# Hybrid decoder layer on one core: opening groups with sums on VectorE, one pool of slots for raw weights, h requested through ScalarE's queue, constants made later

## The chip, the core and the metric

The kernel runs on one core of a Trainium2 chip. Its matrix engine is TensorE (PE in the profile; PEld is its weight load). VectorE (DVE), ScalarE (ACT) and GpSimd (POOL) do the elementwise work, and SyncE (SP) only issues transfers. Each engine takes its instructions in the order of its own queue, and transfers that an engine issues stand in that same queue until their own waits are over. The metric is the time of one execution in microseconds, lower is better.

## The reference

One layer over 256 tokens of width 2048, all in float32: a half-step SwiGLU FFN of inner width 5632 with post-LayerNorm, a mixer (multi-head latent attention and differential attention side by side, merged by sigmoid gates), and a second FFN.

```python
h = _layer_norm(ALPHA * h + 0.5 * _swiglu(h, ffn1_w_gate, ffn1_w_up, ffn1_w_down), ln1_g, ln1_b)
mix = _mixer(h, positions, w_in, ...)
h = _layer_norm(ALPHA * h + mix, ln2_g, ln2_b)
h = _layer_norm(ALPHA * h + 0.5 * _swiglu(h, ffn2_w_gate, ffn2_w_up, ffn2_w_down), ln3_g, ln3_b)

def _swiglu(x, w_gate, w_up, w_down):
    return (jax.nn.silu(x @ w_gate) * (x @ w_up)) @ w_down
```

The mixer needs a few constants: rotary sines and cosines of the positions, a causal mask, distance biases, the scalar lambda and a scaled gain row.

## The kernel before

**Numbers.** Every float32 operand is split in two (`split`, lines 188 to 190): ACT casts it to a high part in float32r, VectorE subtracts that from the source for the low part. A product is three matmuls (`triple`, lines 245 to 248): high by high, high by low, low by high. The stationary operand is a 128x128 tile of x, the moving one 512 columns of weights.

**Units.** Weights come in units of 128x1024 floats (two k tiles of 512 columns, 512 KB). A plain unit is loaded by SP into a raw tile, split into a pair of ring tiles (`wring`), and multiplied with both blocks of 128 tokens: 12 matmuls. Up to 3 units are loaded and 4 split ahead of the one that is multiplied (`look(3, 4)`).

**Groups.** In the FFNs two column chunks, the two token blocks and, for part of the k range, two halves of k are worked by a scheme of seven block products instead of eight (`Pair.seven`). A formed unit multiplies one sum or difference of weight blocks with one sum or difference of x blocks: 6 matmuls. The weight blocks are called A and E (first chunk), B and D (second chunk); each is two units. In the kernel before A, E and D are loaded as `sraw` tiles by SP; where B has to be added, POOL issues an accumulating load of it into the tile in place (line 328), after the tile's split. Other sums are made by VectorE (line 323). The formed x blocks (`Acts.sevens`) are `minus`, a pair from the raw tile, four differences (line 168) and two more pairs.

A gate-and-up group (`group`) is 14 formed units (products 1 to 7, two units each) and 8 plain ones ((chunk, unit) with units 4 to 7). Its products meet in PSUM banks; ACT copies a bank after products 1, 6 and 5 (line 387) and after product 7 (line 392, in `third`), and the copies are combined with the plain units' banks (line 576). In an ordinary group the second half of the units (1, 4) to (1, 7) adds into bank X, which the copy in line 392 reads. Eleven groups make one FFN's gate and up. The first one, `opening=True`, has an order of its own, since x or h is only then arriving; its plain units are multiplied with block 0 at once and with block 1 up to `lag` units later.

**h.** The SwiGLU result is transposed in blocks and written to DRAM (`hT`, line 557). The down stage reads it back in quads of 512 rows (`get`, line 598, `hraw`) by POOL's queue. `seven` in the down stage asks for the quads of a formed block 16 and 14 units ahead and for the quad of its plain units 2 units ahead; `take` asks 11 units ahead.

**Order.** Functions attached by `at(i, ...)` run when unit i is multiplied, or when it is loaded if inline; `later(n, ...)` runs a function n units on. This sets the program's order; a planner then lays out each engine's queue from it by priority, so that work without open inputs can stand earlier. Tiles of 4 KB per partition come from one pool of 40 slots (`act`): ring pairs, x and h quads, sums, snapshots, z, gain rows. Raw weight tiles have a pool of their own with 4 buffers (`wpool`). Six small `tmp` slots serve the rest.

**Constants.** `setup` runs 24 units into the first FFN: it loads positions, frequencies, lambda's vectors and the gain row by POOL's queue and makes the mixer's constants from them on VectorE and ACT.

**LayerNorm.** Its constructor, at the start of a down stage, loads the residual into four z tiles and has ACT scale them 4 units later (line 488); `take_rows` loads gain and bias rows and has ACT halve the gain 4 units later (line 496).

## Time and profile before

| | us |
|---|---|
| median of 3 runs (2122.46 to 2128.14) | 2124.46 |
| profiled execution, whole | 2124.58 |
| its span, first to last instruction | 2122.7 |
| TensorE busy in the span | 2032.3 |
| VectorE busy | 1611.9 |
| ACT busy | 1231.5 |
| first FFN's gate and up | from 0 to about 512 |
| its down stage | about 512 to 754 |
| mixer and output projection | about 754 to 1377 |
| second FFN | about 1377 to 2123 |

A view's row for a group of instructions has line, engine, operation, tiles (out<-in), shape and count, then busy us, mean ns, and the idle time before with what ended it. A timeline row has start and length in us, and in brackets the idle time before and its releaser. A row of stretches has for each engine its busy time and count, then the granted TensorE clock (1.00 is full), the DMA share and GB/s. Where all four token and weight operands pass through one helper, line 189 is ACT's cast and line 190 VectorE's subtraction; tiles tell them apart (raw: plain unit, sraw: formed unit, xs: formed x, hraw: h read back).

### The profile page before, as it was taken

Reading aid. Unit: us, or ns where it says so; the run is one execution under the profiler, and the core shown is the slowest. Engines: PE = TensorE matmul, PEld = TensorE weight load, DVE = VectorE, ACT = ScalarE, POOL = GpSimd, SP = SyncE. Lnnn points to the kernel's source line nnn. Section 1 sums busy time; section 2 is a strip of 40 time slices with the busy share of each in tenths; the row PEclk is TensorE's granted clock in tenths of the full one; section 3 lists DMA queues with packets and bytes.
Section 4 is the critical chain, followed back from the end, with each engine's and each line's share of the span. In section 5 each row is a group of like instructions: output and inputs, shape, how many; then the busy total and the mean of one; then the engine's idle time right before and its main releaser. Section 6 shows DMA issues by size and latency. Waiting matters only on the chain.

```text
span 2122.7 us, 25232 instructions
## 1 busy us (share of the span) xinstructions
PE 2032.3 (96%) x8968; PEld 1659.4 (78%) x8968; DVE 1611.9 (76%) x1905; ACT 1231.5 (58%) x1569; POOL 262.2 (12%) x399
## 2 busy tenths in 40 slices
PE   7789999999999999999999999988999999999997
PEld 5678888887887788888888887866888888787875
DVE  4788888888898885455665555678888888888887
ACT  4566656666665575554674444456656566666563
POOL 1211121122101000000000000011211121221110
PEclk8899999999999999999999999999999999999999
DMA  8767888878878756544455575666888888887983
GB/s 266 188 197 235 228 255 240 236 228 307 273 263 257 243 170 215 175 159 150 168 169 189 189 269 179 215 210 185 228 255 246 233 246 251 249 286 230 290 256 126
DMA packets 135134, 475.16 MB, mean 224 GB/s; under 512 B 17424, under 2 KB 17504, under 8 KB 135008
## 3 DMA queue, kind: packets, MB, share of 16 engines
q1 hardware_dynamic: 100512, 358.13, 48.5%
q0 software_dynamic: 34496, 115.42, 23.8%
q8 instruction: 70, 1.15, 0.2%
q14 instruction: 56, 0.46, 0.1%
HBM read 455.66 MB, written 17.83 MB: 223 GB/s over the span
## 4 chain that ended last, share of the span: by engine, by line
PE 57%; DMA 13%; DVE 11%; issue 9%; ACT 4%; POOL 1%; ACTq 0%; DVEq 0%; SPq 0%; POOLq 0%
PE mm L246 18%; PE mm L248 18%; PE mm L247 18%; DVE wring L190 6%; DMA sraw<-in_gu_dram 5%; DMA hraw<-hT 3%; ACT wring L189 2%; DMA raw<-in_dn_dram 2%; DMA sraw<-in_dn_dram 1%; DVE sraw L323 1%; DMA z<-res 1%; DMA lv<-in_lam_dram 1%; POOL sraw L328 1%; DVE h L190 1%; DMA z<-in_x_dram 0%
## 5 line engine op out<-in xcount | busy, mean ns | idle before, releaser
L190 DVE TENSOR_TENSOR wring<-raw,wring 128x1024 fp32r<-128x1024 f32 (+2 forms) x502 | 601.1, 1205 | 283.3 <-ACT wring L189 282.6
L189 ACT CAST wring<-raw 128x1024 fp32r<-128x1024 f32 (+2 forms) x502 | 515.7, 1038 | 360.0 <-PE mm L248 287.4
L189 ACT CAST wring<-sraw 128x1024 fp32r<-128x1024 f32 x420 | 436.0, 1050 | 295.4 <-DVE sraw L323 101.7
L190 DVE TENSOR_TENSOR wring<-sraw,wring 128x1024 fp32r<-128x1024 f32 x420 | 504.3, 1218 | 102.2 <-ACT wring L189 100.4
L246 PE MATMUL mm<-wring,h 128*128 128x512 f32 (+2 forms) x1344 | 528.1, 393 | 13.3 <-ACT snap L392 5.5
L247 PE MATMUL mm<-wring,h 128*128 128x512 f32 (+2 forms) x1344 | 522.4, 389 | 3.6 <-DVE wring L190 3.5
L248 PE MATMUL mm<-wring,h 128*128 128x512 f32 (+2 forms) x1344 | 521.6, 388 | 0.7 <-DVE h L190 0.4
L246 PE MATMUL mm<-wring,xs 128*128 128x512 f32 x840 | 333.9, 398 | 25.9 <-ACT wring L189 13.8
L247 PE MATMUL mm<-wring,xs 128*128 128x512 f32 x840 | 335.1, 399 | 17.4 <-DVE wring L190 17.3
L248 PE MATMUL mm<-wring,xs 128*128 128x512 f32 x840 | 331.4, 395 | 1.6 <-DVE xs L190 1.5
L246 PEld LDWEIGHTS mm<-wring,h 128*128 128x128 f32 x1344 | 254.6, 189 | 68.1 <-ACT snap L392 7.9
L247 PEld LDWEIGHTS mm<-wring,h 128*128 128x128 f32 x1344 | 254.9, 190 | 56.3 <-DVE wring L190 7.1
L248 PEld LDWEIGHTS mm<-wring,h 128*128 128x128 f32 x1344 | 254.6, 189 | 53.7 <-DVE h L190 2.6
L246 PEld LDWEIGHTS mm<-wring,xs 128*128 128x128 f32 x840 | 160.3, 191 | 66.9 <-ACT wring L189 19.2
L247 PEld LDWEIGHTS mm<-wring,xs 128*128 128x128 f32 x840 | 160.8, 191 | 60.5 <-DVE wring L190 27.1
L248 PEld LDWEIGHTS mm<-wring,xs 128*128 128x128 f32 x840 | 160.6, 191 | 35.0 <-DVE xs L190 2.3
L246 PE MATMUL mm<-wring,x 128*128 128x512 f32 x352 | 139.5, 399 | 10.9 <-ACT snap L392 5.7
L323 DVE TENSOR_TENSOR sraw<-sraw,sraw 128x1024 f32<-128x1024 f32 x120 | 144.0, 1220 | 1.3 <-DMA sraw<-in_gu_dram 0.3
L328 POOL DMA_DIRECT2D sraw<-in_gu_dram x88 | 75.9, 863 | 536.0 <-DMA raw<-in_gu_dram 237.2
L247 PE MATMUL mm<-wring,x 128*128 128x512 f32 x352 | 139.2, 396 | 2.0 <-DVE wring L190 2.0
L248 PE MATMUL mm<-wring,x 128*128 128x512 f32 x352 | 138.9, 395 | 0.0
L557 POOL DMA_DIRECT2D hT<-blocks x176 | 96.9, 559 | 264.9 <-DVE blocks L555 262.1
(250 smaller groups left out, 1775.5 us busy)
## 6 DMA issues: line engine op xcount, KB each, us to landing
raw<-in_gu_dram SPq DMA_DIRECT2D x176, 512.0 KB, 4.6
sraw<-in_gu_dram SPq DMA_DIRECT2D x132, 512.0 KB, 7.0
raw<-in_dn_dram SPq DMA_DIRECT2D x112, 512.0 KB, 4.4
sraw<-in_gu_dram POOLq DMA_DIRECT2D x88, 512.0 KB, 8.0
sraw<-in_dn_dram SPq DMA_DIRECT2D x48, 512.0 KB, 6.2
hraw<-hT POOLq DMA_DIRECT2D x44, 512.0 KB, 10.1
sraw<-in_dn_dram POOLq DMA_DIRECT2D x32, 512.0 KB, 7.2
raw<-in_wgm_dram SPq DMA_DIRECT2D x32, 512.0 KB, 3.3
```

What stands on the lines that cost most here:

```text
L189: S.copy(hi, src)
L190: V.tensor_tensor(out=lo, in0=src, in1=hi.bitcast(F32), op=ALU.subtract)
L246: PE.matmul(o, xh, wh, start=first, stop=False, skip_group_check=again)
L247: PE.matmul(o, xh, wl, start=False, stop=False, skip_group_check=again)
L248: PE.matmul(o, xl, wh, start=False, stop=last, skip_group_check=again)
L323: V.tensor_tensor(out=t, in0=t, in1=self.blocks[joins[p], s], op=ALU.add)
L328: nc.gpsimd.dma_start(self.blocks[adds[p], s], self.w[1][4 * d + s], accum_op=ALU.add)
L557: nc.gpsimd.dma_start(hT[q, b].rearrange("(g r) (i f) -> i r g f", g=4, i=4)[i], t[32 * i:32 * (i + 1), :].rearrange("r (g f) -> r g f", g=4))
```

## The change

- Opening groups (both FFNs): B is loaded by SP into two tiles of its own, and VectorE adds it into A before product 5 and into D before product 7; no accumulating loads there. Six plain units come first, then products mixed with the two others. Just before product 1 all delayed block-1 products are made (`together`, `lag` 0), and x's formed blocks and the later x loads move by one to four units.
- Ordinary groups: product 7 and the unit (0, 7) change places, and the second of the four outputs is finished by that unit and no longer by `third`.
- Raw tiles come from the common pool, now 44 slots; `wpool` and its 4 buffers are gone.
- `get` is issued by ACT instead of POOL, 18, 16 and 8 units ahead for formed blocks and their plain units, 16 for `take`.
- z is scaled 16 units after its load in the FFNs and 5 in the mixer's end, the gain rows 10 units after.
- `setup` runs at the start of the first FFN's second half of down; it keeps the mask and issues all loads, and `constants` makes the rest 16 units later.

```diff
@@ -29,7 +29,7 @@
 G = 2
-SLOTS = 40
+SLOTS = 44
 LAG = 5
@@ -62,7 +62,6 @@
     const = ctx.enter_context(tc.tile_pool(name="const", bufs=1))
-    wpool = ctx.enter_context(tc.tile_pool(name="wpool", bufs=1))
     apool = ctx.enter_context(tc.tile_pool(name="apool", bufs=1))
@@ -267,7 +266,7 @@
             def load():
-                st["raw"] = wpool.tile([P, G * width], F32, tag="raw", name=nm("raw"), bufs=4)
+                st["raw"] = act_tile([P, G * width], F32, "raw")
                 nc.sync.dma_start(st["raw"], w[j])
@@ -303,11 +302,14 @@
 
-        def seven(self, d, p, then=None):
+        def seven(self, d, p, then=None, by_dma=True):
             fresh = {1: ("A", 0, 0), 2: ("E", 0, 2), 3: ("D", 1, 2)}
...
             joins = {6: "D", 4: "E"}
-            adds = {1: "A", 6: "D"}
+            adds = {1: "A", 6: "D"} if by_dma else {}
+            if not by_dma:
+                fresh[5] = ("B", 1, 0)
+                joins.update({5: "B", 7: "B"})
 
@@ -347,7 +349,7 @@
             def load():
-                st["raw"] = wpool.tile([P, 1024], F32, tag="raw", name=nm("raw"), bufs=4)
+                st["raw"] = act_tile([P, 1024], F32, "raw")
                 nc.sync.dma_start(st["raw"], self.w[n][j])
@@ -394,16 +396,14 @@
                 done(0, 0, bk["Y"], n1, ALU.subtract)
-            done(0, 1, bk["W"], n3, ALU.subtract)
-            if opening:
+                done(0, 1, bk["W"], n3, ALU.subtract)
                 done(1, 0, bk["Z"], n2, ALU.add)
...
         def last0(b):
-            if b == 0:
-                done(0, 0, bk["Y"], st["t"][0], ALU.subtract)
+            done(0, b, bk["YW"[b]], st["t"][2 * b], ALU.subtract)
 
@@ -412,13 +412,13 @@
         if opening:
-            seq = [(0, 4), (0, 5), (1, 4), (1, 5), (0, 6), 1, (1, 6), 2, (0, 7), 5, (1, 7), 3, 6, 4, 7]
+            seq = [(0, 4), (0, 5), (1, 4), (1, 5), (0, 6), (1, 6), 1, (0, 7), 2, (1, 7), 5, 3, 6, 4, 7]
         else:
-            seq = [1, 2, (0, 4), 5, (0, 5), 3, 6, (0, 6), 4, (0, 7), 7, (1, 4), (1, 5), (1, 6), (1, 7)]
+            seq = [1, 2, (0, 4), 5, (0, 5), 3, 6, (0, 6), 4, 7, (0, 7), (1, 4), (1, 5), (1, 6), (1, 7)]
         items = []
...
             if isinstance(i, int):
-                items += pr.seven(0, i, thens.get(i))
+                items += pr.seven(0, i, thens.get(i), not opening)
             else:
@@ -485,7 +485,7 @@
                     nc.gpsimd.dma_start(t, residual[b, :, h * 1024:(h + 1) * 1024])
-                    later(4, lambda t=t: S.mul(t, t, ALPHA))
+                    later(16 if scale < 1.0 else 5, lambda t=t: S.mul(t, t, ALPHA))
             self.rows = (g, bt)
@@ -493,7 +493,7 @@
             for t in self.gb[0]:
-                later(4, lambda t=t: S.mul(t, t, 0.5))
+                later(10, lambda t=t: S.mul(t, t, 0.5))
 
@@ -585,7 +585,12 @@
                            lambda n_, b, bank, snap, op, p=p: sum_done(2 * p + n_, b, bank, snap, op), p == 0)
-        for i, f in zip((5, 7, 10, 11, 13), x.sevens(0)):
+        def together():
+            lag[0] = 0
+            catch_up(0)
+
+        at(6, together)
+        for i, f in zip((6, 8, 11, 12, 13), x.sevens(0)):
             at(i, f)
@@ -595,13 +600,13 @@
         def get(i, q):
-            nc.gpsimd.dma_start(hx[i].raw(q), hT[q].rearrange("b p f -> p b f"))
+            nc.scalar.dma_start(hx[i].raw(q), hT[q].rearrange("b p f -> p b f"))
 
...
         def take(i, q):
-            at(len(items) - 11, lambda: get(i, q))
+            at(len(items) - 16, lambda: get(i, q))
             for b in range(2):
@@ -649,11 +654,11 @@
                 t = len(items)
-                at(t - 16, lambda: get(i, 2 * d))
-                at(t - 14, lambda: get(i, 2 * d + 1))
+                at(t - 18, lambda: get(i, 2 * d))
+                at(t - 16, lambda: get(i, 2 * d + 1))
                 for k, f in enumerate(hx_forms(i, d)):
                     at(t - 7 + k, f)
-                at(t - 2, lambda: get(i, q))
+                at(t - 8, lambda: get(i, q))
                 for b in range(2):
@@ -679,6 +684,8 @@
             else:
+                if n == 1:
+                    at(len(items), setup)
                 items += lone(4)
@@ -728,12 +735,20 @@
         nc.gpsimd.dma_start(pos_i, a["pos_col"])
+        row_i = tmp_tile([P, T], "row_i", I32)
+        nc.gpsimd.dma_start(row_i, a["pos_row"].partition_broadcast(P))
+        invf = tmp_tile([P, HALF], "invf")
+        nc.gpsimd.dma_start(invf, a["inv_freq"].partition_broadcast(P))
+        lv = tmp_tile([P, 4, P], "lv")
+        nc.gpsimd.dma_start(lv.rearrange("p a n -> p (a n)"), a["lam"].partition_broadcast(P))
+        nc.gpsimd.dma_start(subg, a["subln_g"].partition_broadcast(P))
+        later(16, lambda: constants(pos_i, row_i, invf, lv))
+
+    def constants(pos_i, row_i, invf, lv):
         pos = sm(2, "pos")
...
         V.tensor_scalar(out=npos, in0=pos, scalar1=-1.0, scalar2=None, op0=ALU.mult)
-        row_i = tmp_tile([P, T], "row_i", I32)
-        nc.gpsimd.dma_start(row_i, a["pos_row"].partition_broadcast(P))
         row = tmp_tile([P, T], "posrow")
@@ -743,8 +758,6 @@
 
-        invf = tmp_tile([P, HALF], "invf")
-        nc.gpsimd.dma_start(invf, a["inv_freq"].partition_broadcast(P))
         ang = tmp_tile([P, 2, 2, HALF], "ang")
@@ -763,8 +776,6 @@
 
-        lv = tmp_tile([P, 4, P], "lv")
-        nc.gpsimd.dma_start(lv.rearrange("p a n -> p (a n)"), a["lam"].partition_broadcast(P))
         lp = tmp_tile([P, 2, P], "lp")
@@ -774,7 +785,6 @@
         V.tensor_scalar(out=lam, in0=ld, scalar1=LAMBDA_INIT, scalar2=None, op0=ALU.add)
-        nc.gpsimd.dma_start(subg, a["subln_g"].partition_broadcast(P))
         V.tensor_scalar(out=subg, in0=subg, scalar1=0.5 * (1.0 - LAMBDA_INIT), scalar2=None, op0=ALU.mult)
@@ -1044,10 +1054,9 @@
     def first(at):
-        for i, q, b in ((0, 2, 0), (1, 2, 1), (4, 3, 0), (4, 3, 1), (5, 0, 0), (5, 0, 1), (5, 1, 0), (5, 1, 1)):
+        for i, q, b in ((0, 2, 0), (1, 2, 1), (4, 3, 0), (4, 3, 1), (6, 0, 0), (8, 1, 0), (8, 1, 1), (9, 0, 1)):
             at(i, lambda q=q, b=b: load_x(q, b), True)
 
-    later(24, setup)
     set_ring(LAG + 5)
...
```

## Prediction

> **What bounds the kernel now.** I read the page's engine shares first, then the stretches, then the waits of TensorE, then the timelines of the holes.
>
> ```profile
> span 2122.7 us, 25232 instructions
> PE 2032.3 (96%) x8968; PEld 1659.4 (78%) x8968; DVE 1611.9 (76%) x1905; ACT 1231.5 (58%) x1569; POOL 262.2 (12%) x399
> 300.00:350.00 50.00, 50.00 (x222) 41.42 (x221) 43.80 (x48) 31.79 (x38) 11.84 (x20) 1.00 0.80 230
> 25.00:50.00 25.00, 17.56 (x51) 11.43 (x52) 13.64 (x14) 10.19 (x12) 1.74 (x2) 0.73 0.70 202
> 50.00:75.00 25.00, 20.08 (x78) 15.04 (x78) 21.95 (x21) 16.46 (x20) 3.36 (x4) 0.93 0.63 175
> 75.00:100.00 25.00, 17.43 (x65) 13.16 (x64) 19.12 (x31) 11.55 (x16) 7.83 (x13) 0.85 0.79 215
> 100.00:125.00 25.00, 20.48 (x73) 15.97 (x72) 18.49 (x35) 15.81 (x18) 0.00 (x0) 0.81 0.53 149
> 1400.00:1425.00 25.00, 21.93 (x92) 17.18 (x91) 20.31 (x21) 15.47 (x17) 1.68 (x2) 0.98 0.84 272
> 1425.00:1450.00 25.00, 22.56 (x86) 17.56 (x85) 19.49 (x22) 16.50 (x20) 1.69 (x2) 0.89 0.59 133
> 1450.00:1475.00 25.00, 20.27 (x77) 15.39 (x78) 21.04 (x22) 11.93 (x13) 6.17 (x10) 0.93 0.71 212
> ```
>
> The columns after the stretch are its length, then busy time and count on PE, PEld, DVE, ACT and POOL, then the granted clock, the DMA share and GB/s. A steady stretch holds 222 matmuls in 50 us, one per 0.225 us: there TensorE is the bound and nothing but fewer matmuls would help, and the change keeps their number. So the time that can move is in stretches with fewer matmuls. Against 111 per 25 us, the stretches from 25 to 125 us lack 60, 33, 46 and 38, which at 0.225 us is 13.5, 7.4, 10.4 and 8.6 us; those from 1400 lack 19, 25 and 34 (4.3, 5.6, 7.7 us). A hole costs more than its width: the granted clock falls to 0.73 to 0.93 with it.
>
> **The change, part by part.** The sum is made against the profiled execution, 2124.58 us, which is the span and 1.9 us around it; the median of the runs shown, 2124.46, is the same.
>
> *a. The third snapshot no longer stands before a matmul.* In an ordinary group the copy of bank X (line 392) is followed at once by the unit (1,4), whose second half adds into X. The new order puts the 12 matmuls of (0,7) between.
>
> ```profile
>   PE mm L246: 11.2, 6
> 497.26 0.39 PE L248 MATMUL mm<-wring,x 128*128 128x512 f32 x1
> 501.59 0.50 PE L246 MATMUL mm<-wring,x 128*128 128x512 f32 x1 [3.94 <-ACT snap L392]
> 502.56 0.63 PE L246 MATMUL mm<-wring,x 128*128 128x512 f32 x1
> 505.11 0.63 PE L246 MATMUL mm<-wring,x 128*128 128x512 f32 x1
> 490.81 1.06 ACT L488 ACTIVATE z<-z 128x1024 f32<-128x1024 f32 x1 [3.25 <-DMA z<-in_x_dram]
> 498.77 1.05 ACT L488 ACTIVATE z<-z 128x1024 f32<-128x1024 f32 x1
> 500.96 0.58 ACT L392 COPY snap<-mm 128x512 f32<-128x512 f32 x1
> ```
>
> The first row is from the view of line 392: TensorE lost 11.2 us to it in 6 waits. In the longest one shown, six matmuls from 502.56 to 505.11 then took 2.55 us, 1.2 us over pace; two such long waits (the second FFN repeats the first's code) make at most 11.2 + 3 = 14. The copy came late because ACT stood 3.25 us for the residual tile z and then scaled four of them at about 1.06 us each. These scalings move from 4 units to 16 units behind the load, out of the last group, so 7 us of what kept ACT late goes too. What is late next is the cast of the following unit, right behind the copy on ACT. Gain 3 (that cast takes the place) to 14; I take 11, since both causes go.
>
> *b. Constants leave the first FFN's second group.*
>
> ```profile
> 97.27 0.68 DVE L751 TENSOR_SCALAR ang<-invf,pos 128x32 f32<-128x32 f32 x4 [3.30 <-DMA invf<-in_inv_freq_dram]
> 107.77 0.43 DVE L769 TENSOR_TENSOR lp<-lv 128x256 f32<-128x256 f32 x1 [4.61 <-DMA lv<-in_lam_dram]
> L761 DVE SCALAR_TENSOR_TENSOR ang<-turns,ang 128x128 f32<-128x128 f32 x12 | 3.4, 283 | 0.0
> L743 DVE SCALAR_TENSOR_TENSOR bias<-dist,mask 128x384 f32<-128x384 f32 x4 | 2.0, 554 | 0.2 <-ACT dist L741 0.2
> 103.63 1.05 ACT L189 CAST wring<-sraw 128x1024 fp32r<-128x1024 f32 x1 [7.36 <-DMA sraw<-in_gu_dram]
> ```
>
> VectorE stood 7.9 us for two small loads with splits queued behind, and did 3.4 + 2.0 us and some 4 us of smaller constants, together about 9.5. The stretches 75 to 125 lost 19.0 us; the second FFN's like group, without constants, lost 7.7. So the gain is at most 11.3; at least 0, as the cast at 103.63 waited 7.36 us for an added block which the constants did not hold up. I take 8, nearer the comparison.
>
> The work returns in the first FFN's down stage, where VectorE is close to full:
>
> ```profile
> 600.00:650.00 50.00, 50.00 (x222) 41.41 (x221) 46.69 (x55) 28.92 (x34) 4.69 (x6) 1.00 0.85 283
> 650.00:700.00 50.00, 47.09 (x198) 37.74 (x197) 42.35 (x43) 30.98 (x36) 7.25 (x10) 0.97 0.83 252
> ```
>
> It has 3.3 + 7.7 = 11 us free in these 100 us, against 9.5 of work. The loads now go out 16 units ahead, so they have landed. On POOL's queue they stand ahead of that stage's accumulating loads, five issues of under 0.9 us each (the row of L598 below bounds one at 1.09). Hidden, the cost is 0; without cover 9.5. I take 3. ACT has 19 us free per 50 for its few functions and table loads.
>
> *c and d. The two opening groups.* They lose four accumulating loads each (POOL) and gain two plain ones (SP) and four adds on VectorE.
>
> ```profile
> L323 DVE TENSOR_TENSOR sraw<-sraw,sraw 128x1024 f32<-128x1024 f32 x29 | 34.8, 1220 | 0.2
> 21.62 0.90 SPq L318 DMA_DIRECT2D sraw<-in_gu_dram  x2
> 37.84 0.33 SPq L351 DMA_DIRECT2D raw<-in_gu_dram  x1
> SPq L351 <- DVE wring L190: 1210.2, 258, 31.6
> 34.08 1.04 ACT L189 CAST wring<-sraw 128x1024 fp32r<-128x1024 f32 x1 [4.23 <-DMA sraw<-in_gu_dram]
> 1387.72 0.40 PE L248 MATMUL mm<-wring,h 128*128 128x512 f32 x1
> 1394.89 0.79 PE L246 MATMUL mm<-wring,xs 128*128 128x512 f32 x1 [6.77 <-ACT xs L189]
> L190 DVE TENSOR_TENSOR wring<-sraw,wring 128x1024 fp32r<-128x1024 f32 x20 | 23.7, 1220 | 4.4 <-ACT wring L189 4.4
> ```
>
> The four later x loads also move behind the first formed tiles on SP's queue, so those tiles arrive sooner and half of x up to four units later, just ahead of the formed unit that reads it. Price: 4 x 1.22 = 4.9 us of VectorE per opening, against 13.64 busy of 25 in the first hole, so it fits there. Gain in the first FFN: SP issued nothing from 22.5 to 37.8 us, since its next load was a raw tile and all four raw buffers were full, while ACT waited up to 4.23 us for tiles queued behind. Raw tiles taken from all 44 slots lift that, and the six plain units give 72 matmuls (16 us) before any formed block is needed. The loss there is 20.9 us (25 to 75). But a formed unit of 6 matmuls is 1.35 us of TensorE and 1.22 of VectorE for its split, and eight of the fourteen now carry an add: their 14 x 1.22 + 8 x 1.22 = 26.8 us are more than their 18.9 us of matmuls. VectorE becomes the bound of the rest of the opening. Gain 2 to 15; I take 8.
>
> In the second FFN the hole of 6.77 us at 1387.7 is block 1's matmuls standing behind the first formed unit, which waits for its negated input. The new order runs six plain units' first halves, then all six second halves (36 matmuls, 8.1 us), before it; block 1's own normalisation is then late next. Those fillers are gone afterwards, when VectorE, already 20.31 and 19.49 busy of 25, gets 4.9 more. Loss 3 to gain 12; I take a gain of 6.
>
> *e. h by ACT's queue, 2 to 6 units sooner.*
>
> ```profile
> L598 POOL DMA_DIRECT2D hraw<-hT x44: 709/1044/1087, 478.9 to 2060.7; - x44
> DMA to landing us min/median/max: 7.4/10.1/16.0
> raw<-in_gu_dram SPq DMA_DIRECT2D x176, 512.0 KB, 4.6
> 686.12 1.14 ACT L189 CAST h<-hraw 128x512 fp32r<-128x512 f32 x2 [5.89 <-DMA hraw<-hT]
> 688.26 0.50 PE L246 MATMUL mm<-wring,h 128*128 128x512 f32 x1 [1.76 <-ACT wring L189]
> 689.52 0.50 PE L247 MATMUL mm<-wring,h 128*128 128x512 f32 x1 [0.76 <-DVE wring L190]
> 2000.00:2050.00 50.00, 46.18 (x197) 36.85 (x196) 42.37 (x43) 32.49 (x39) 6.37 (x9) 0.98 0.86 267
> ```
>
> The down stages' late stretches lack 24 and 25 matmuls (5.4 and 5.6 us). The cause in the first is a cast that stood 5.89 us for h. The request moves from 2 units ahead to 8, at least 6 x 1.35 = 8.1 us, more than that wait. Each issue costs ACT between 0.33 (SP's row) and 1.04 us (POOL's), 15 to 46 us in all; ACT's 17 to 19 idle us per 50 cover it; if a request finds its slot taken, ACT stops, with the casts behind it, and TensorE waits for those. POOL's queue loses 44 issues, so its accumulating loads go out sooner. Loss 4 to gain 11; I take 7.
>
> The Trainium skill's DMA: Bandwidth & Descriptors, section Issuing engines are not separate DMA queues, speaks against a part of this: all issuers share the same 16 engines, and another issuer saves only issue time. The rows differ for the two queues, 10.1 against 4.6 us, though for different sources. By the rule only the earlier request counts and I would put e at 5, the sum at 2090; by the rows 2088.
>
> Sum: -11 - 8 + 3 - 8 - 6 - 7 = -37, so 2087.6, say **2088 us**. With the ends above taken not all together, its own range is 2068 to 2106.
>
> **The rivals.**
>
> *R1, VectorE takes over.* The openings and the down stage merely move from load waits to VectorE: b and c and d give 4 in place of 22, less 3, a and e stay at 11 and half of 7. Speaks for it: 26.8 us of VectorE against 18.9 us of matmuls. Against: VectorE idle for 11.4 of 25 us in the first hole. 11 + 4 + 3.5 - 3 = 15.5, so 2109.
>
> *R2, slower: raw loads crowd out the others.* SP waited 1210.2 us on raw buffers, so it is always ready to run ahead; with a common pool it can fill every slot, and then each group's snapshot tiles wait for a split to release one. Place: the snapshot copy on ACT, with casts behind it. A release comes per unit, up to 12 x 0.225 = 2.7 us. In 22 groups (11 pairs in each FFN) that is up to 59 us, against my 37: 2147. It decides from 1.7 us per group. Against: 40 + 4 slots were there before as well. The same end has ACT stopped by a request whose slot is not free: 5.89 us, the wait seen, in each of eight formed blocks is 47, less 37: 2135.
>
> *R3, nearly nothing.* Sharing does not let SP run ahead, because the planned order holds it, and b, c and d only shift waits: a and half of e, less the whole 9.5 of constants, is 5 us: 2120.
>
> *R4, all holes close:* 14 + 11.3 + 15 + 12 + 11 - 3 = 60: 2064.
>
> **How the numbers follow.** Forecast 0.46; R1 0.17; R4 0.13; R3 0.09; R2 with its twin 0.15. What a measurement can tell here is about 0.3%, 6.4 us, so no change is 2118 to 2131. Faster is forecast, R1 and R4, 0.76; same 0.08, nearly all of R3; slower 0.16, R2 and the rest. The range runs from under R4 to the edge of no change, 2058 to 2130, and leaves out R2 and a little of R4.
>
> **What would show it.** Right: no wait of TensorE for line 392 over 1 us; no idle VectorE for invf or lv; SP issuing between 22 and 37 us, and the stretch 25 to 50 us with over 80 matmuls; no hole of 6 us near 1390; hraw landing under 8 us and no cast waiting over 2 us for it; 600 to 700 us with no fewer than 415 matmuls. Wrong: steady stretches under 218 matmuls per 50 us, SP or ACT waiting on snapshot releases (R2), or ACT idle just before a request for h.

## The result, and the profile after

| | before | after |
|---|---|---|
| median of 4 runs, us | 2124.55 | 2196.60 |
| lowest to highest | 2122.46 to 2128.14 | 2193.89 to 2205.74 |
| span of the profiled execution | 2122.7 | 2204.0 |
| first FFN, to the first transposition of its LayerNorm | 754.1 | 721.1 |
| mixer and output projection, to that of the second | 620.3 | 746.1 |
| second FFN, the rest of the span | 748.3 | 736.8 |

The kernel after takes 1.0345 times as long, with an interval of 1.0312 to 1.0378. The forecast was 2088 us and its range ended at 2130, so it was wrong, and in sign. (The profiled execution of the kernel after is the longest of its four, 9.1 us above their median; the phases are those of that execution.) The two FFNs together gained 44.5 us, more than the 37 that the prediction had summed for them. The mixer, for which the prediction had no term at all, lost 125.8 us.

From the page of the kernel after, the span and the engine shares:

```profile
span 2204.0 us, 25328 instructions
PE 2064.4 (94%) x8968; PEld 1676.3 (76%) x8968; DVE 1615.7 (73%) x1913; ACT 1226.5 (56%) x1569; POOL 224.0 (10%) x347
```

TensorE has the same 8968 matmuls, VectorE eight more instructions (the eight adds), and POOL 52 fewer. No engine has more to do than before: TensorE's busy time grew by 32.1 us, but for the same matmuls, at a mean granted clock of 0.970 instead of 0.982. The rest of the 81.3 us between the spans is waiting, and a wait has a place. I cut the span where TensorE transposes z in the LayerNorms. The rows for z in the first half and in the second half of the span, first of after and then of before (the last two numbers ahead of the shape are the first and last start, in us):

```profile
L430 PE MATMUL tr<-ident,z x32: 270/272/421, 721.1 to 748.0; 128*128 128x128 f32 x32
L430 PE MATMUL tr<-ident,z x32: 270/272/273, 1467.2 to 1490.1; 128*128 128x128 f32 x32
```

```profile
L430 PE MATMUL tr<-ident,z x32: 272/273/301, 754.1 to 768.2; 128*128 128x128 f32 x32
L430 PE MATMUL tr<-ident,z x32: 270/272/275, 1374.4 to 1387.1; 128*128 128x128 f32 x32
```

The first start of each is the cut: 721.1 and 1467.2 after, 754.1 and 1374.4 before. All tables below are cut in this way, each from one profiled execution.

The stretches of the kernel after that answer to those of the prediction, and one of the mixer (columns as there: length, then busy time and count on PE, PEld, DVE, ACT, POOL, then granted clock, DMA share, GB/s):

```profile
25.00:50.00 25.00, 20.15 (x77) 14.91 (x75) 17.30 (x18) 11.33 (x12) 0.00 (x0) 0.93 0.75 290
50.00:75.00 25.00, 21.20 (x75) 15.73 (x76) 21.25 (x21) 13.81 (x16) 1.80 (x2) 0.86 0.72 203
75.00:100.00 25.00, 18.88 (x73) 14.17 (x72) 20.05 (x23) 13.37 (x17) 6.22 (x10) 0.93 0.63 165
100.00:125.00 25.00, 25.00 (x112) 20.69 (x111) 21.74 (x26) 18.15 (x23) 3.23 (x5) 1.00 0.93 308
300.00:350.00 50.00, 50.00 (x221) 41.13 (x220) 43.26 (x44) 33.19 (x39) 7.95 (x12) 1.00 0.84 257
600.00:650.00 50.00, 47.89 (x206) 38.19 (x206) 44.67 (x64) 30.74 (x37) 3.47 (x4) 1.00 0.77 225
650.00:700.00 50.00, 47.30 (x200) 36.48 (x199) 48.47 (x62) 37.13 (x43) 5.62 (x8) 1.00 0.83 267
850.00:900.00 50.00, 38.94 (x155) 28.96 (x154) 15.91 (x18) 19.04 (x27) 0.00 (x0) 0.88 0.30 100
```

The stretch of the same times in the kernel before, also in its mixer:

```profile
850.00:900.00 50.00, 50.00 (x245) 41.40 (x244) 23.46 (x25) 29.32 (x42) 0.00 (x0) 1.00 0.52 169
```

The four opening stretches hold 337 matmuls against 267 (70 x 0.225 = 15.8 us won). The FFN's ordinary groups are as steady as before, 221 against 222. In the mixer's stretch 155 matmuls stand where there were 245, TensorE has holes, and nothing else is busy: VectorE 15.91 of 50, ACT 19.04, the DMA share 0.30. A stretch in which TensorE stands and every other engine is idle most of the time is not short of any engine; something may stand in the wrong order. The whole mixer, first after and then before:

```profile
721.10:1467.20 746.10, 666.56 (x2930) 537.57 (x2929) 357.83 (x535) 329.27 (x495) 9.17 (x17) 0.94 0.45 157
754.10:1374.40 620.30, 617.23 (x2929) 515.32 (x2929) 361.04 (x536) 334.21 (x494) 9.19 (x17) 1.00 0.56 187
```

Of the 125.8 us, 76.5 are idle time of TensorE (79.54 against 3.07); the other 49.3 are longer busy time for the same matmuls, at a granted clock of 0.94 against 1.00.

The waits of TensorE in the whole span, first after and then before (total us, times, longest):

```profile
PE mm L245 <- ACT wring L188: 79.0, 34, 7.3
PE mm L246 <- DVE wring L189: 37.3, 51, 4.9
PE mm L245 <- ACT snap L389: 0.7, 1, 0.7
```

```profile
PE mm L247 <- DVE wring L190: 22.8, 26, 3.4
PE mm L246 <- ACT wring L189: 22.3, 14, 4.3
```

(Lines moved up by one: 188 and 189 after are 189 and 190 before.) The waits for a snapshot, 11.2 and 2.9 us before, are down to 0.7. The waits for a cast of weights went from 22.3 to 79.0 us; 59.1 of these, in 25 waits, lie in the mixer, where the kernel before has none. A place in the mixer shows what they wait for. ACT and TensorE of the kernel after at the end of one projection, from their timelines:

```profile
837.94 1.05 ACT L188 CAST wring<-raw 128x1024 fp32r<-128x1024 f32 x1 [1.67 <-PE mm L247]
847.46 0.59 ACT L881 COPY dqTr<-mm 128x512 f32<-128x512 f32 x1 [8.47 <-PE mm L247]
851.55 0.59 ACT L881 COPY dqTr<-mm 128x512 f32<-128x512 f32 x1 [3.50 <-PE mm L247]
852.03 0.59 ACT L806 COPY dqT<-tr 128x512 f32<-128x512 f32 x1
853.82 0.58 ACT L806 COPY dqT<-tr 128x512 f32<-128x512 f32 x1 [1.20 <-PE tr L805]
854.30 2.00 ACT L188 CAST wring<-raw 128x1024 fp32r<-128x1024 f32 x2
```

```profile
853.18 0.60 PE L805 MATMUL tr<-ident,dqTr 128*128 128x128 f32 x4
855.40 0.73 PE L245 MATMUL mm<-wring,cn 128*128 128x512 f32 x2 [1.62 <-ACT wring L188]
856.66 0.71 PE L246 MATMUL mm<-wring,cn 128*128 128x512 f32 x1 [0.53 <-DVE wring L189]
```

ACT of the kernel before at the like place:

```profile
851.99 0.59 ACT L871 COPY dqTr<-mm 128x512 f32<-128x512 f32 x1 [0.30 <-PE mm L248]
853.35 1.05 ACT L189 CAST wring<-raw 128x1024 fp32r<-128x1024 f32 x1 [0.77 <-PE mm L248]
856.07 0.58 ACT L871 COPY dqTr<-mm 128x512 f32<-128x512 f32 x1 [1.67 <-PE mm L248]
```

Before, a cast of a coming unit stands between the copies that empty the projection's banks. After, from 838.99, the end of the first row, to 854.30 ACT makes no cast at all: it stands 8.47 us for a bank that TensorE is still filling, and the next weights' casts are queued behind that copy and the three that follow it. When the transposition at 853.18 is done, TensorE has nothing split, stops for 1.62 and 0.53 us, and takes the next matmuls at half pace (0.43 us apart for a while).

### The profile page after: what moved, and what is told of

It is laid out like the page before. It is cut to its first block, busy times and chain, and to the rows that moved or that the text cites. A ratio compares the mean times of both kernels' runs of the same rounds, so it can differ in the third digit from the quotient of the medians.

```text
span 2204.0 us, 25328 instructions
## 1 busy us (share of the span) xinstructions
PE 2064.4 (94%) x8968; PEld 1676.3 (76%) x8968; DVE 1615.7 (73%) x1913; ACT 1226.5 (56%) x1569; POOL 224.0 (10%) x347
## 3 DMA queue, kind: packets, MB, share of 16 engines
q0 software_dynamic: 27008, 88.15, 18.9%
## 5 line engine op out<-in xcount | busy, mean ns | idle before, releaser
L189 DVE TENSOR_TENSOR wring<-raw,wring 128x1024 fp32r<-128x1024 f32 (+2 forms) x502 | 589.1, 1206 | 276.2 <-ACT wring L188 274.0
L188 ACT CAST wring<-raw 128x1024 fp32r<-128x1024 f32 (+2 forms) x502 | 503.0, 1036 | 149.4 <-PE mm L247 135.7
L246 PE MATMUL mm<-wring,h 128*128 128x512 f32 (+2 forms) x1344 | 529.4, 394 | 11.6 <-DVE wring L189 11.3
L245 PEld LDWEIGHTS mm<-wring,h 128*128 128x128 f32 x1344 | 256.9, 192 | 96.2 <-ACT wring L188 43.4
L246 PEld LDWEIGHTS mm<-wring,h 128*128 128x128 f32 x1344 | 258.2, 192 | 72.0 <-DVE wring L189 21.2
L247 PEld LDWEIGHTS mm<-wring,h 128*128 128x128 f32 x1344 | 258.2, 192 | 53.4 <-DVE h L189 2.2
L325 DVE TENSOR_TENSOR sraw<-sraw,sraw 128x1024 f32<-128x1024 f32 x128 | 153.3, 1220 | 0.9
L330 POOL DMA_DIRECT2D sraw<-in_gu_dram x80 | 70.6, 892 | 484.6 <-DVE wring L189 335.6
```

What stands on the lines that cost most here:

```text
L188: S.copy(hi, src)
L189: V.tensor_tensor(out=lo, in0=src, in1=hi.bitcast(F32), op=ALU.subtract)
L245: PE.matmul(o, xh, wh, start=first, stop=False, skip_group_check=again)
L246: PE.matmul(o, xh, wl, start=False, stop=False, skip_group_check=again)
L247: PE.matmul(o, xl, wh, start=False, stop=last, skip_group_check=again)
L325: V.tensor_tensor(out=t, in0=t, in1=self.blocks[joins[p], s], op=ALU.add)
```

## The experiments

Two theories of the mixer's loss are named in the expectations. **T1**: sharing changed the *order* in the queues. Raw tiles with buffers of their own could be loaded and cast ahead of other tiles that the program asks for earlier; tiles of a common pool are not, and the mixer's program asks for each unit only when it is due (its lookahead is 0, 0). **T2**: sharing changed the *capacity*: raw tiles take slots that others then lack. R1 to R4 are the prediction's rivals.

All results, with the phases cut as above:

| kernel | median us | ratio to before, interval | first FFN | mixer | second FFN |
|---|---|---|---|---|---|
| before | 2124.55 | | 754.1 | 620.3 | 748.3 |
| after | 2196.60 | 1.0345 (1.0312 to 1.0378) | 721.1 | 746.1 | 736.8 |
| after, raw tiles in their own buffers | 2170.89 | 1.0210 (1.0188 to 1.0232) | 768.0 | 621.9 | 778.0 |
| ... and product 7 in its old place | 2096.98 | 0.9846 (0.9822 to 0.9869) | 735.6 | 622.0 | 738.8 |
| before + sharing alone | 2236.21 | 1.0510 (1.0481 to 1.0539) | 739.7 | 741.0 | 751.1 |
| before + product 7 moved alone | 2192.64 | 1.0297 (1.0265 to 1.0328) | 785.7 | 620.2 | 784.2 |
| before + h by ACT alone | 2102.24 | 0.9873 (0.9852 to 0.9893) | 743.6 | 621.8 | 735.7 |
| before + constants moved alone | 2117.66 | 0.9938 (0.9916 to 0.9960) | 744.2 | 621.6 | 753.1 |
| before + openings alone | 2133.20 | 1.0017 (1.0006 to 1.0029) | 761.7 | 622.9 | 755.0 |
| before + later scalings alone | 2128.14 | 1.0001 (0.9990 to 1.0012) | 756.0 | 620.3 | 753.5 |
| after + lookahead in the mixer | 2091.65 | 0.9829 (0.9809 to 0.9850) | 717.2 | 639.5 | 734.5 |
| after + lookahead from FFN to FFN | 2068.97 | 0.9717 (0.9694 to 0.9740) | 718.2 | 621.8 | 724.6 |
| ... with the old openings | 2070.91 | 0.9719 (0.9705 to 0.9734) | 723.4 | 623.0 | 722.8 |

Ratios stand against runs of the kernel before on the same chip (medians 2128.27, 2129.22 and 2128.38 in the three sets). Each phase is read from one execution. With the constants alone, no edit touches the second FFN, and it still differs by 4.8 us from the kernel before; so a difference of 5 us in one phase says nothing by itself.

### Raw tiles back in their own buffers

```diff
-SLOTS = 44
+SLOTS = 40
+    wpool = ctx.enter_context(tc.tile_pool(name="wpool", bufs=1))
...
-                st["raw"] = act_tile([P, G * width], F32, "raw")
+                st["raw"] = wpool.tile([P, G * width], F32, tag="raw", name=nm("raw"), bufs=4)
...
-                st["raw"] = act_tile([P, 1024], F32, "raw")
+                st["raw"] = wpool.tile([P, 1024], F32, tag="raw", name=nm("raw"), bufs=4)
```

> The change with one part undone: raw tiles are back in a pool of their own with 4 buffers, the common pool back at 40 slots. From the first FFN's LayerNorm (first transposition of z) to the second one's lie 620 us in the kernel before and 746 us in the changed one; the first FFN got 33 us shorter. T1 (a raw tile of the common pool is not placed ahead of the other tiles that stand before it in the program, so in the mixer, whose units have no lookahead in program order, loads and casts bunch behind the evacuations) and T2 (44 slots are too few in the mixer once raw tiles take their share) both expect the mixer back at 620 +- 10 us and 2085 us in all. T3 (another part, such as the constants made late or h on ACT's queue, spoils the mixer) expects it to stay over 720 and the whole over 2180 us.

The mixer is back at 621.9 us: its loss belongs to sharing and to nothing else of the change. But the whole is still 2170.89, since both FFNs now lose, 47 and 41 us against the kernel after. So a second cost lay in the change, and sharing hid it. It is a stop of 1.7 to 3.8 us that recurs in 18 of the 20 ordinary groups. TensorE, ACT and POOL of this kernel in one of them, from the timelines:

```profile
152.86 0.50 PE L246 MATMUL mm<-wring,xs 128*128 128x512 f32 x1 [2.84 <-ACT wring L189]
```

```profile
146.37 1.05 ACT L189 CAST wring<-sraw 128x1024 fp32r<-128x1024 f32 x1 [4.39 <-DMA sraw<-in_gu_dram]
150.81 1.99 ACT L189 CAST wring<-sraw 128x1024 fp32r<-128x1024 f32 x2 [3.39 <-DMA sraw<-in_gu_dram]
```

```profile
137.70 0.93 POOL L331 DMA_DIRECT2D sraw<-in_gu_dram  x1 [2.09 <-issue]
138.84 0.87 POOL L331 DMA_DIRECT2D sraw<-in_gu_dram  x1 [0.21 <-ACT snap L390]
```

By the buffer numbers in the program's queues, the three casts are these:

```
146.37  cast of D, first unit of product 7    waits for POOL's load at 137.70 (landed 146.3)
150.81  cast of D, second unit of product 7   waits for POOL's load at 138.84 (landed 150.7)
151.76  cast of A, second unit of product 4   its sum was ready at 145.3
```

TensorE wants product 4's second unit and gets it 2.84 us late, because its cast stands on ACT behind both casts of product 7, which wait for the accumulating loads of B into D.

### Product 7 back in its old place as well

```diff
-            seq = [1, 2, (0, 4), 5, (0, 5), 3, 6, (0, 6), 4, 7, (0, 7), (1, 4), (1, 5), (1, 6), (1, 7)]
+            seq = [1, 2, (0, 4), 5, (0, 5), 3, 6, (0, 6), 4, (0, 7), 7, (1, 4), (1, 5), (1, 6), (1, 7)]
```

(The second of the four outputs is finished in `third` again.)

> The changed kernel with raw tiles back in a pool of their own (4 buffers, 40 common slots, as in e1_own_pool) and the ordinary groups' old order, (0, 7) before product 7. In e1_own_pool each ordinary group loses 3 to 5 us at the first formed unit after the five plain units in a row that the new order makes, and the first FFN takes 768 us against 754 before. T4 (five raw loads in a row do not fit 4 buffers, so the next group's A stands behind them on SP's queue) expects that loss to go: first FFN 725 to 740, second 735 to 750, the whole 2095 to 2110 us. The rival (the loss per group is from something else of the change, such as the h requests or fewer free slots) expects 765 and over 2160 us.

73.9 us come back, 32.4 in the first FFN and 39.2 in the second. What is left of the change (openings, constants, h, scalings) makes the kernel before faster by 1.5%. The expectation (T4) put the cost of the moved product on the five plain units that now follow each other, with four raw buffers for them, and its time came out. Its mechanism did not: it wants the stop at the first formed unit behind the plain ones, and the trace of the kernel above, with product 7 moved, has it ahead of them, at product 4. Behind 154.31 TensorE waits for nothing until 198.51, where the next group's product 4 stops in the same way. In both kernels SP issues the same five loads just ahead of POOL's, and POOL's land as late (9.0 and 12.1 us in the old order); what differs is how soon product 7 needs them.

### Product 7 moved alone

The reverse of the last diff, in the kernel before.

> The kernel before with one part of the change alone: in ordinary groups product 7 comes before (0, 7). The prediction's step a expects 11 us less, 2113 us. T4 expects the snapshot waits gone, but 3 to 5 us lost in each of 20 ordinary groups: 2170 to 2210 us.

```profile
PE mm L246 <- ACT wring L189: 56.7, 34, 4.0
```

It alone costs 63 us, all of it in the FFNs (+31.6 and +35.9), and the wait for casts, 22.3 us before, is 56.7. In the kernel after, the move costs nothing to be seen (221 matmuls per 50 us). The casts of product 7 stand ahead of product 4's second unit there too, but POOL's loads land sooner. ACT and POOL of the kernel after in a group:

```profile
338.90 1.05 ACT L188 CAST wring<-sraw 128x1024 fp32r<-128x1024 f32 x1 [1.31 <-PE mm L247]
342.29 2.00 ACT L188 CAST wring<-sraw 128x1024 fp32r<-128x1024 f32 x2 [2.33 <-DMA sraw<-in_gu_dram]
```

```profile
333.31 0.94 POOL L330 DMA_DIRECT2D sraw<-in_gu_dram  x1 [2.11 <-issue]
335.45 0.89 POOL L330 DMA_DIRECT2D sraw<-in_gu_dram  x1 [1.21 <-ACT wring L188]
```

The two loads landed at 338.7 and 342.2, so 5.4 and 6.8 us after their issue, against 8.6 and 11.9 us with raw tiles in their own buffers. With those, SP had issued five loads of 512 KB in the four microseconds before; with the common pool it issued two in ten. The other groups repeat this: over the 20 ordinary groups the first of the two loads lands in the median after 5.4 us and the second after 6.9 in the kernel after, 5.4 and 7.0 with sharing alone, 8.6 and 11.0 in the kernel before, and 8.7 and 11.0 with product 7 moved alone. The kernel before holds both cases: in 16 groups five of SP's loads go out in the four microseconds before, and the first load lands after 8.4 to 10.0 us; in the last group of each FFN one goes out, and it lands after 5.4. That the company of SP's loads makes the difference is the likely reading; no run changed that alone.

### Sharing alone

The first diff reversed, in the kernel before (44 slots, both raw tiles from the common pool).

> The kernel before with one part of the change alone: raw tiles from the common pool, 44 slots. T1 and T2 expect the mixer at 720 to 750 us and the whole over 2210 us, worse than the change itself, since nothing else gains. T3 expects 2124 us, no change.

The mixer takes 741.0 us: +120.7 of the 125.8. The first FFN gains 14.4, the second loses 2.8.

### Lookahead in the mixer, raw tiles still shared

```diff
     def mixer(x):
+        look(2, 2)
...
-                later(5 + 3 * h + 2 * i, f)
+                later(9 + 3 * h + 2 * i, f)
...
-                later(4 + 6 * h + 3 * i, f)
+                later(8 + 6 * h + 3 * i, f)
...
-            catch_up(0)
-            for t in (g0, g1):
-                S.activation(t, t, AF.Sigmoid)
+            def sigmoids():
+                catch_up(0)
+                for t in (g0, g1):
+                    S.activation(t, t, AF.Sigmoid)
+            doing.append(sigmoids)
...
+        look(0, 0)
         return yq
```

The program now asks for two units and splits two ahead of the one that is multiplied; the rest of the diff keeps what depends on a unit behind it.

> The change with its shared pool as it is, and one edit in the mixer: its units are loaded and split up to 2 units each ahead in the program's order, as in the FFNs (the gates' sigmoids move to the first unit that needs them, heads start 4 units later to keep their place). T1 expects the mixer back at 620 to 640 us and the whole at 2085 to 2100 us. T2, where slots are short whatever the order, expects the mixer over 700 us and the whole over 2160 us.

The mixer falls from 746.1 to 639.5 us with the same 44 shared slots, and the kernel to 2091.65. Capacity did not change, order did: T1 holds and T2 falls. Holes are left where the lookahead is emptied, among them one at the mixer's start and one ahead of the output projection:

```profile
728.18 0.79 PE L245 MATMUL mm<-wring,h 128*128 128x512 f32 x1 [5.62 <-ACT wring L188]
1270.37 1.22 PE L245 MATMUL mm<-wring,y 128*128 128x512 f32 x2 [7.29 <-ACT wring L188]
```

### Lookahead kept from the first FFN to the second

```diff
     def mixer(x):
-        look(2, 2)
...
-        look(0, 0)
         return yq
...
-    look(0, 0)
+    look(2, 2)

     yq = mixer(h1)
-    catch_up(0)
-    flush()
```

> The kernel of e4_lookahead with the lookahead kept on from the end of the first FFN to the second FFN's opening, without emptying it between. Its three largest holes stood just where the lookahead was emptied: 11.8 us at the mixer's start, 11.5 at the output projection's start, 10 at the second opening. T1 expects most of the first two to go: mixer 615 to 625 us in place of 639.5, the whole 2060 to 2078 us. If those holes are from the LayerNorm or from the slots, it stays within 6 us of 2091.7.

```profile
850.00:900.00 50.00, 50.00 (x242) 41.72 (x241) 22.51 (x31) 27.50 (x44) 0.00 (x0) 1.00 0.43 149
1255.00:1280.00 25.00, 25.00 (x116) 20.75 (x115) 18.78 (x20) 13.21 (x14) 0.00 (x0) 1.00 0.73 282
```

Both stretches are full, the mixer takes 621.8 us and the kernel 2068.97: 2.8% below the kernel before, the lowest median here. This is the change as it was meant, with its order mended.

### 40 slots shared

```diff
-SLOTS = 44
+SLOTS = 40
```

> The change with the common pool cut from 44 to 40 slots, raw tiles still in it. T2 expects the mixer to get clearly worse, over 780 us against 746, and the whole over 2235 us. T1 expects it within 15 us of 746, and the whole within 25 us of 2197 us, since what holds the raw tiles back is their place in the program and not their number.

One time, 2221.16 us, 24.6 above the kernel after: inside what T1 allowed, by a hair, and below what T2 wanted. Another execution took 4171.27 us; the record does not show why, and it is left out, and with it the profile, which is its own. Alone, this time decides little. A larger pool was not tried.

### h by ACT's queue, alone

```diff
-            nc.gpsimd.dma_start(hx[i].raw(q), hT[q].rearrange("b p f -> p b f"))
+            nc.scalar.dma_start(hx[i].raw(q), hT[q].rearrange("b p f -> p b f"))
...
-            at(len(items) - 11, lambda: get(i, q))
+            at(len(items) - 16, lambda: get(i, q))
...
-                at(t - 16, lambda: get(i, 2 * d))
-                at(t - 14, lambda: get(i, 2 * d + 1))
+                at(t - 18, lambda: get(i, 2 * d))
+                at(t - 16, lambda: get(i, 2 * d + 1))
...
-                at(t - 2, lambda: get(i, q))
+                at(t - 8, lambda: get(i, q))
```

> The kernel before with one part of the change alone: h is asked for on ACT's queue, 2 to 6 units sooner. The prediction's step e expects 7 us less, 2117 us, with bounds of 11 less and 4 more; no cast should wait over 2 us for h. If the rule that issuers only differ in issue time holds fully, the landing stays near 10.1 us in the median; by the rows it falls under 8.

The rows for hraw and two stretches of its first down stage:

```profile
L598 ACTq DMA_DIRECT2D hraw<-hT x44: 366/366/768, 471.3 to 2037.2; - x44
DMA to landing us min/median/max: 3.6/6.3/12.5
650.00:700.00 50.00, 49.08 (x216) 39.98 (x215) 44.18 (x45) 34.74 (x39) 6.48 (x9) 1.00 0.89 274
700.00:750.00 50.00, 48.45 (x220) 39.22 (x219) 46.81 (x60) 33.12 (x47) 0.00 (x0) 1.00 0.67 215
```

The second of those stretches in the kernel before:

```profile
700.00:750.00 50.00, 46.10 (x191) 36.26 (x190) 42.04 (x47) 28.16 (x31) 3.08 (x4) 0.97 0.72 225
```

27.0 us, 10.5 and 12.6 of it in the FFNs' phases by the profile. It is the largest gain of any single part. Stretches of 198 and 191 matmuls now have 216 and 220. In the kernel before, ACT waited 47.5 us for h in 13 waits, up to 6.37 us; here it waits for h nowhere.

### Constants in the down stage, alone

`setup` moved to the first FFN's second half of down, its loads first and `constants` 16 units later, as in the change's diff.

> The kernel before with one part of the change alone: setup and the constants made in the first FFN's down stage. The prediction's step b expects the first FFN's gate and up 8 us shorter (0 to 11.3) and its down stage 3 us longer (0 to 9.5): 2123 us in all, 5 us less. If the down stage has no room on VectorE, its two late 50 us stretches lose 9.5 us and the whole is not faster.

```profile
75.00:100.00 25.00, 21.93 (x82) 16.95 (x80) 20.48 (x23) 12.00 (x16) 6.19 (x10) 0.86 0.77 208
100.00:125.00 25.00, 24.55 (x108) 20.26 (x109) 20.15 (x23) 16.35 (x22) 1.69 (x2) 1.00 0.83 243
650.00:700.00 50.00, 45.11 (x185) 35.69 (x184) 44.18 (x65) 36.36 (x42) 8.51 (x12) 0.93 0.80 241
```

Against 65 and 73 matmuls, the group has 82 and 108: 52 x 0.225 = 11.7 us. The down stretch falls from 198 to 185, 2.9 us. By the medians 10.7 us are won; the interval of the ratio makes it 8.5 to 17.9.

### The openings, alone

B on SP's queue, the eight adds on VectorE, the new order and `together`, without the rest.

> The kernel before with one part of the change alone: the opening groups, with B loaded by itself and added on VectorE, six plain units first, and the delayed block-1 products made at once. The prediction's steps c and d expect 8 and 6 us less, 2114 us, with bounds of 27 less and 1 more. The rival T4' (more plain units in a row meet 4 raw buffers here too, so the gain needs the shared pool) expects no gain or a loss in the openings.

```profile
100.00:125.00 25.00, 18.32 (x58) 13.77 (x59) 22.70 (x44) 15.41 (x18) 2.89 (x4) 0.80 0.61 172
PE mm L247 <- DVE wring L190: 34.0, 36, 3.7
```

No gain: 0.17% slower. The stretch that still holds the constants drops from 73 to 58 matmuls with VectorE busy 22.70 of 25, and the waits for VectorE's splits go from 22.8 to 34.0 us.

### The old openings in the best kernel

The opening parts undone in the kernel with lookahead throughout.

> The kernel of g2_lookahead_through (2069.0 us) with the opening groups of the kernel before. If the opening's gain needs the shared pool (T4'), it is slower than g2 by the 14 us of the prediction's steps c and d, 2075 to 2090 us, although g5 alone shows no gain. If the new opening costs time in any surroundings, this one is faster than g2.

2070.91 against 2068.97, which is no difference. The phases (5.2 us more in the first FFN, 1.8 less in the second) differ by no more than phases do by themselves. So the 14 us that the openings were to win in the company of shared raw tiles (T4' in the expectations) are not there either.

### The later scalings, alone

```diff
-                    later(4, lambda t=t: S.mul(t, t, ALPHA))
+                    later(16 if scale < 1.0 else 5, lambda t=t: S.mul(t, t, ALPHA))
...
-                later(4, lambda t=t: S.mul(t, t, 0.5))
+                later(10, lambda t=t: S.mul(t, t, 0.5))
```

> The kernel before with one part of the change alone: the residual tiles z are scaled 16 units after their load (5 at the mixer's end), the gain rows 10 units after. The prediction put this under step a as half of the reason why the copy in line 392 comes late at the end of each gate and up: it expects the two longest waits of TensorE there (3.9 and 5.1 us, with their slow clock about 12 us) to shrink to under 1 us, 2113 to 2118 us. If the copy is late for its place in ACT's queue alone, nothing changes.

1.0001. TensorE's long waits for line 392 stay (4.48 and 5.56 us, at 501.62 and 1860.16). But the edit did not clear the place: of the four scalings two still stand ahead of the copy, which starts at 500.99, and ACT still waits for the first tile z (3.65 us, against 3.25 in the kernel before).

```profile
490.70 1.06 ACT L488 ACTIVATE z<-z 128x1024 f32<-128x1024 f32 x1 [3.65 <-DMA z<-in_x_dram]
492.94 1.06 ACT L488 ACTIVATE z<-z 128x1024 f32<-128x1024 f32 x1 [0.24 <-DMA z<-in_x_dram]
```

So this run does not tell what the scalings cost. The kernel with own raw buffers and product 7 in its old place tells more: there one scaling stands ahead of the copy and none waits for z, and TensorE still waits 3.66 and 3.78 us for the copy, behind casts that wait 3.16 and 2.26 us for the down stage's weights.

## Why the prediction was wrong

**The missing term.** The step that failed is a term put at nothing: the sum had none for sharing raw tiles outside the openings, where it was booked as a gain. Sharing was weighed in one place only, R2, and there dismissed with "40 + 4 slots were there before as well". That sentence counts capacity, and capacity was not what moved. R2 named the right part, but put its price on snapshots in 22 FFN groups (59 us); those groups kept 221 matmuls per 50 us. The 125.8 us were lost between 754 and 1377 us, in stretches that the prediction never read: it looked for stretches with *few* matmuls, in which time could be won, and not at the full ones, in which it could be lost. A row of the mixer (245 matmuls in 50 us, with a lookahead of 0 in the program) asks what lets it run ahead; the answer was the four buffers that the change takes away.

**Step a** (-11, of 3 to 14). The waits for the third snapshot did go, from 11.2 us to none (0.7 us are left for the others). The size and the sign were wrong: the move alone costs 63 us. The step asked what is late next, answered with the cast of the unit behind the copy, and let that lower the gain to 3 at worst. The unit that got *earlier* by the swap was not followed: product 7 reads D with B added, and came 12 matmuls, 2.7 us, nearer to two loads that land 8.6 and 11.9 us after issue. That the scalings kept ACT late was at most a part of it: with one of four left ahead of the copy, waits of 3.66 and 3.78 us stayed. How large a part stays open.

**Step b** (-8 and +3). Right in mechanism and near in size. The group won 11.7 us, just over the upper end of 0 to 11.3, and the down stretch paid 2.9, put at 3.

**Steps c and d** (-8 and -6). Alone +4.8 us, in company no difference. The step itself had worked out that VectorE needs 26.8 us against 18.9 us of matmuls and took a gain all the same; R1's reason, VectorE as the openings' bound, was the better account of them (its price for the constants was too low). The first FFN's four opening stretches did win 70 matmuls, but most of these came without the new opening: with the old one the best kernel has 327 there, 60 more than the kernel before, against 343. No hole of 6 us is left in the second opening (the longest wait is 4.69 us, at 1477.21), and the runs that change the openings alone do not show its phase shorter.

**Step e** (-7, at most 11). The mechanism was right and the size was off: 27.0 us. The term was made from two stretches, 650 to 700 and 2000 to 2050; the two behind them lacked as many (191 and 196 matmuls in 700 to 750 and 2050 to 2100), and the first of these rose to 220 by the same edit. An issue on ACT took 0.37 us where POOL took 1.04. The median landing fell from 10.1 to 6.3 us (7.2 in the kernel after). By the Trainium skill's DMA: Bandwidth & Descriptors, section Issuing engines are not separate DMA queues, another issuer saves only the issue time. A landing is counted here from the start of its issue, so it holds the 0.7 us by which the issue got shorter; the other 3.1 us of the fall are more than that rule gives. The runs changed queue and request together and can't part them. Other company on the 16 engines at the earlier time could be the cause; that is not shown.

**Together.** With neither sharing nor the swap the change gave 32 us (2096.98), where b to e had been put at 26. That these agree is luck: e gave 20 us more than its term, and the openings fell 19 short of theirs. The two edits beside it, one booked as a gain and one as free, cost 63 and 126 us where they stand unmended. Of the signs named, the gone waits for line 392, VectorE's for invf and lv, SP's loads between 22 and 37 us, the landing of h under 8 us (7.2), no cast waiting for h and the missing hole of 6 us came true; 25 to 50 us has 77 matmuls in place of 80, and 600 to 700 us 406 in place of 415. The sign for "wrong", stretches under 218 matmuls, appeared in the mixer.

**Why the two costs don't add.** Alone sharing costs 108 us and the swap 63, together with gains of 33 this would be +138; the kernel after stands at +72. By the landings above, shared raw tiles take away what makes the swap dear, so the swap's cost shows only where sharing is undone. A single undoing (2170.89) would have said that sharing costs 26 us; the phases said 124 in the mixer and -88 in the FFNs.

## What to carry to other kernels

A buffer that a tile has to itself is also a licence to run ahead of the program's order. Before a prefetch tile is moved into a common pool, look at every stage whose program asks for it only when due, full ones above all, and write the lookahead into the program first. When units change places, follow the one that comes sooner to the loads it reads, and read the phases of an undone part, not its total: two parts of one change can hide each other.

## What was not expected of the hardware

A DMA issue took 0.37 us on ACT's queue and 1.04 us on POOL's for the same transfer of 512 KB. The same accumulating loads landed in 5.4 and 6.8 us or in 8.6 and 11.9 us after issue, in groups that do the same work, with two of SP's loads issued in the ten microseconds before them or with five in four. And many short holes cost much more than their width: behind a stop of 1.62 us the matmuls came 0.43 us apart instead of 0.23, and over the mixer 76.5 us more of idle time came with 49.3 us more of busy time for the same matmuls.
